# Other durations, and table loads, in the clock by which a two-block kernel lays out its background steps

## The chip, the cores and the metric

The kernel runs on one core of a Trainium2 chip. The metric is the device time of one execution in microseconds, the median of several runs. Names of engines: PE is the matrix engine (TensorE), PEld its weight loads, DVE is VectorE, ACT is ScalarE, POOL is GpSimd and SP is SyncE, which issues the transfers of the weights.

## The reference, cut to what matters

Two transformer-like blocks work one after the other on a sequence of 512 tokens with 1024 features, all in float32. A block adds a mixer and then a gated feed-forward (SwiGLU) to its input, each behind a root-mean-square norm.

```
x   : [1, 512, 1024]
first block, layer 0:  HGRN2 mixer, 8 heads of 128 keys and 128 values:
    S_t = diag(f_t) S_{t-1} + (1 - f_t) i_t^T ;  o_t = S_t^T q_t
    o = rmsnorm(o) * silu(g) ;  h = x + o @ w_out ;  h = h + swiglu(rmsnorm(h))
first block, layer 1:  dilated window attention, 12 heads in 3 groups, softmax over the groups,
    then swiglu
second block:  two mixers side by side on one input
    NSA: 8 query heads of 64 in 2 groups; three branches (compressed keys, selected blocks, window),
         each softmax(q k + mask) v, weighted by a sigmoid gate and added
    GLA: 4 heads, gated linear attention with forget factors exp(logsigmoid(.)/16)
    mix = sigmoid(m1) * (GLA out @ upg) + sigmoid(m2) * (NSA out @ upn) ;  h = h + mix @ wout2
    then swiglu
out : [512, 1024]
```

## The kernel before

**The weights.** All weight matrices pass through once, 187 MB, in units of 128 x 1024 numbers (`w_raw`). ACT casts each unit to a rounded head (`w_hi`), and the rest (`w_lo`) is a subtraction, on DVE for even units and on POOL for odd ones (line 278). A product of a weight block with an operand that is itself kept as head and rest is three matmuls of 512 columns (`mm3`): here this is called a weight product. The program has 2747 of them, and their order is fixed: HGRN's projections (operand `u`) and its output projection (`og`), feed-forward, attention, feed-forward, then the second block's projections (`u`), the products that take GLA's output (`obh`, `obl`) and those that take NSA's (`oan`), output, feed-forward.

**The background steps.** What the mixers do beside the weights (scores, decays, softmax, values) is written as generators. `spawn` puts one on a list; after every weight product `tick` lets at most one of them lay out its next step. A step's instructions on PE, DVE, ACT and POOL then stand in those engines' queues at that place for good: this is decided while the program is built.

**The clock.** `tick` asks a model of the engines, `Clock`. Every engine call goes through `Timed` (line 228, which is why each row of the trace has that line), and `Clock.issue` adds `Clock.cost` to that engine's model time, after the model times of what the instruction reads and writes, plus a hop of 0.5 us between engines (0.55 in the second block). A step is laid out only when the model says that its inputs are there:

```
        for ent in self.bg:
            if ent[1] <= now and ent[3] <= free and all(f() for f in ent[2]):
                return self.step(ent)
```

`now` is PE's model time. **Forced steps.** When a weight product needs an operand that the background has not yet made, `fetch` calls `force` until it is there. Such steps are laid out one behind the other whatever the clock says, with no weight products between them:

```
            while force and not have():
                self.force()
```

**The steps which matter here.** HGRN runs in four pairs of heads (`decay4`: tiles `Q`, `K`, `Sd`, level by level; then `decay_out`: state `St`, values `V`, squares `o_sq`, the root `hrn`, transposes `cst,o`, and `done` writes `o_n`). The output projection takes the heads in order, four output tiles at a time, so heads 6 and 7 are wanted at its 25th product. GLA runs in two pairs (`decay2`: `GQ`, `GK`, seven levels). The second block's compressed branch has steps with `Pc` and `PcT`. NSA's other two branches are 16 jobs (4 pairs of heads x 2 x 2 branches) in one generator, `nsa`: a job's scores (`ks,qs`; then DVE's maxima, and ACT's exponentials into `P`), the sums and gates onto `P` (DVE), its transposes (`cst,P`) into head and rest `PT` (ACT casts, DVE subtracts), and its value products (`PT,VV`). In a round the scores of job n are laid out, then the gates of n-1, the values of n-2, and the transposes of n-1. After every fourth job ACT copies the upper half of a bank (`pv`), DVE adds (`nsum`), POOL adds the compressed branch, and ACT casts the head of `oan`.

Of the kernel before, what the change touches and what calls it, by code (L numbers as in the profile page):

```python
# [24 lines left out]
# columns of the packed per-feature vectors  # L25
# [10 lines left out]
# columns of the constants that stay  # L36
# [9 lines left out]
# the pairs of heads before which HGRN's value products for heads 0..3 and 4..7 come  # L46
HGRN_V = {0: 0, 2: 1}
# attention's sections: the queries and keys of a head of each group, the values of a group's heads
# [4 lines left out]
def nsa_rows():  # L53
    """Feature order of the NSA heads: tile j holds head j of group 0 and head j of group 1."""
    return np.concatenate([np.arange((e * 4 + j) * 64, (e * 4 + j) * 64 + 64) for j in range(4) for e in range(2)])


def attn_heads():
    """(head of the group, group) in the order in which the output projection takes them."""
    return [(t, g) for t in range(4) for g in (1, 2)] + [(t, 0) for t in range(4)]  # L60


def weight_plan():
    """The order in which weight blocks are used: (section, [(matrix, k tile, columns)])."""
# [74 lines left out]
def plan_units(sec, chunks):  # L139
    """Cut a section's blocks into units of at most UNIT columns; the first ones are small, to start early."""  # L140
    units, cur, w = [], [], 0
    for i, ch in enumerate(chunks):
        n = len(ch[2])
        if w + n > UNIT or (sec == "hgrn" and w and i <= KD):
            units.append((cur, w))
            cur, w = [], 0
        cur.append(ch)
        w += n
    if cur:
        units.append((cur, w))  # L150
    return units
# [10 lines left out]

class Clock:
    """Rough times of the engines' queues and of the tiles' contents while the program is laid out:
    they say when a background step's inputs and banks will be there, so that TensorE isn't made to wait."""

    def __init__(self, hop):
        self.hop = hop  # from an instruction's end to the start of another engine's that waits for it
        self.free = {"pe": 0.0, "v": 0.0, "a": 0.0, "g": 0.0}
        self.written, self.read = {}, {}  # L170
        self.held = []

# [3 lines left out]
    def banks(self, now):  # L176
        """PSUM banks that are free by then."""
# [6 lines left out]
    def cost(self, eng, op, out, ins):  # L184
        n = 1
        for d in out.shape[1:]:
            n *= d
# [6 lines left out]
        if eng == "a":  # L194
            return 0.09 + n * 0.00085
        if eng == "g":
            return 0.13 + n * 0.0023
        if op == "reciprocal":
            return 0.06 + n * 0.0064
        return 0.08 + n * (0.00075 if op == "tensor_scalar" else 0.00104)  # L200

    def issue(self, eng, op, outs, ins):
# [10 lines left out]
        t += self.cost(eng, op, outs[0], ins)  # L213
# [6 lines left out]
class Timed:  # L220
# [3 lines left out]
    def __getattr__(self, op):  # L224
        f = getattr(self.eng, op)

        def call(*args, **kw):
# [6 lines left out]
            self.clock.issue(self.name, op, outs, aps + ins)  # L234
# [5 lines left out]
class Weights:  # L240
    """Streams the weights in the order of use and splits each into its float32r head and rest."""
# [70 lines left out]
class Program:  # L312
# [74 lines left out]
    def mm3(self, out, a, b, first, last):  # L387
        """out += a^T b for operands given as (head, rest)."""
# [18 lines left out]
    def gemm(self, xs, M, evac, lead=1, ms=None):  # L407
        """Feature-major product: evac(m, [128 features, 512 tokens]) for each output tile m.
        An operand may be a pair of functions: whether it is there, and what makes it."""
# [13 lines left out]
    def gemm_tok(self, n, residue=False, before=None, after=None, every=1):  # L423
        """Token-major product with n weight columns: four banks of 128 tokens, by blocks or by the rest of the token mod 4."""
# [24 lines left out]
    def norm_feed(self, k, squares=True):  # L449
        """x[k] is final: build the operand's parts and add its squares."""  # L450
# [25 lines left out]
    def sums(self, out, acc, residue=False):  # L476
        """Each token's sum over the partitions of acc, onto the token's partition."""
# [33 lines left out]
    def bcast(self, col, ps=None):  # L511
        """[128 tokens, n] to the first 128 n columns of a PSUM bank that hold every token's value on all partitions."""
# [50 lines left out]
    #  # L563
    # A head's score of query t and key s <= t is q_t . (forget factors of s+1..t) k_s. Keys and queries meet
    # block by block: when neighbouring blocks of h tokens are joined, the queries carry the factors from their
    # block's start, the keys those to their block's end and T holds each block's product, so that every factor
    # is a product of forget factors and nothing is divided.
# [5 lines left out]
    def decay4(self, Q, K, T, have, Vj, done):  # L573
        """Two heads whose values are there when have() says so, with keys K[e] [128, 512] and forget
        factors T [128, 2, 512]; Q[e] [128, 2, 512] holds head e's queries and,
        beside them, room. Blocks are joined four at a time: the room takes the queries that reach back further
        than the block before theirs, with the factors of the blocks between.
        Vj(e, j) gives head e's values of tokens 128 j.. as [tokens, 128]; done(e, o) takes the normed output,
        not yet times its gain."""
        v, a, g = self.v, self.a, self.g  # L580
        # per level: each block's product, and the products of the blocks after each of the first three
# [25 lines left out]
        def begin(e, h, T):  # L607
            """The room's queries for blocks of h tokens."""
# [57 lines left out]
    def decay2(self, Q, K, T, Vj, done):  # L666
        """Two heads on one set of keys K and forget factors T [128, 1, 512], whose queries Q [128, 2, 512] are
        zero outside each head's features. Blocks are joined two at a time."""
# [39 lines left out]
    def decay_out(self, Q, K, T, Sd, have, Vj, done):  # L708
        """Sd holds the scores within each block of 128 tokens. The blocks before come through a state
        [features, values] that is carried from block to block."""  # L710
# [49 lines left out]
    def hgrn(self):  # L760
# [16 lines left out]
        # TensorE's clock is released by activity: these run while the first operands are on their way  # L777
# [99 lines left out]
    def attn(self):  # L877
# [13 lines left out]
        def scores(gi, q, k, st):  # L891
            """Masked scores and their exponentials of one head, four blocks of 128 queries."""
# [27 lines left out]
        def merge(hg, st):  # L920
            """Softmax over the three groups' log-sum-exps, then the weighted outputs."""
# [109 lines left out]
    def block2(self):  # L1031
# [28 lines left out]
        # compressed keys and values  # L1060
# [30 lines left out]
        # gated linear attention operands  # L1091
# [25 lines left out]
        # token-major columns  # L1117
# [62 lines left out]
        # sparse attention  # L1180
# [4 lines left out]
        def rope(raw, i):  # L1185
            """Rotate, then stack the parts of the 64 features for products in two passes: q as head on one
            half of the partitions and rest on the other, k's head on both halves and k's rest on both."""
# [92 lines left out]
        def w_stage(j, e, br, P, l):  # L1280
            """Softmax's sum and the branch's gate, onto the rows of P."""
# [370 lines left out]
```

## Time and profile before

| what | value |
|---|---|
| median of 3 runs | 2163.72 us (2163.47 to 2164.20) |
| span of the profiled execution | 2162.1 us |
| PE busy | 2117.4 us, 98% |
| DVE, ACT, POOL busy | 1004.3, 783.8, 723.6 us |
| mean granted PE clock | 0.994 |

The span goes from the first to the last instruction of one profiled execution. That execution has no time of its own in the results; the runs' median is 1.6 us above the span, so 1.6 us are taken to lie around it.

### The profile page before, as it was taken

Reading aid. Unit: us, or ns where it says so; the run is one execution under the profiler, and the core shown is the slowest. Engines: PE = TensorE matmul, PEld = TensorE weight load, DVE = VectorE, ACT = ScalarE, POOL = GpSimd, SP = SyncE. Lnnn points to the kernel's source line nnn. Section 1 sums busy time; section 2 is a strip of 40 time slices with the busy share of each in tenths; the row PEclk is TensorE's granted clock in tenths of the full one; section 3 lists DMA queues with packets and bytes.
Section 4 is the critical chain, followed back from the end, with each engine's and each line's share of the span. In section 5 each row is a group of like instructions: output and inputs, shape, how many; then the busy total and the mean of one; then the engine's idle time right before and its main releaser. Section 6 shows DMA issues by size and latency. Waiting matters only on the chain.

```text
span 2162.1 us, 25412 instructions
## 1 busy us (share of the span) xinstructions
PE 2117.4 (98%) x9983; PEld 1773.4 (82%) x9983; DVE 1004.3 (46%) x1775; ACT 783.8 (36%) x1290; POOL 723.6 (33%) x442
## 2 busy tenths in 40 slices
PE   9999999999999999999999999999899999999998
PEld 7787788888888998788888888887688788888887
DVE  4778853322334555643322333447778753222322
ACT  5343443222233433443222224244455543222233
POOL 4413343323333434323322335331511253322333
PEclk9999999999999999999999999999999999999999
DMA  5111233323323222222332232321111223333332
GB/s 178 59 59 49 69 127 98 98 98 98 98 88 107 79 88 78 79 69 98 98 102 93 98 98 92 133 69 48 55 55 57 70 95 98 98 98 98 96 100 69
DMA packets 55865, 191.00 MB, mean 88 GB/s; under 512 B 6257, under 2 KB 8321, under 8 KB 55745
## 3 DMA queue, kind: packets, MB, share of 16 engines
q1 hardware_dynamic: 53584, 183.85, 26.2%
q0 software_dynamic: 1008, 3.42, 0.4%
q10 hardware_dynamic: 1152, 2.10, 0.3%
q8 instruction: 78, 1.28, 0.2%
q14 instruction: 43, 0.34, 0.1%
HBM read 187.25 MB, written 2.10 MB: 88 GB/s over the span
## 4 chain that ended last, share of the span: by engine, by line
PE 86%; DVE 9%; issue 1%; POOL 1%; ACT 1%; DMA 1%; SPq 0%; DVEq 0%; ACTq 0%; POOLq 0%
PE ps L228 86%; DVE Q L228 2%; DVE Sd L228 2%; DVE P L228 1%; DMA w_raw<-in_hgrn 1%; DVE w_lo L228 1%; DVE K L228 0%; POOL rot L228 0%; DVE Pc L228 0%; DVE qs L228 0%; POOL rs L228 0%; DVE obl L228 0%; DVE GQ L228 0%; DVE PT L228 0%; POOL w_lo L228 0%
## 5 line engine op out<-in xcount | busy, mean ns | idle before, releaser
L228 PE MATMUL ps<-u,w_hi 128*128 128x512 f32 x3392 | 1049.4, 391 | 0.0
L228 PEld LDWEIGHTS ps<-u,w_hi 128*128 128x128 f32 x3392 | 638.9, 188 | 128.9 <-issue 1.4
L228 PE MATMUL ps<-u,w_lo 128*128 128x512 f32 x1696 | 683.7, 403 | 2.2 <-POOL w_lo L228 2.2
L228 POOL TENSOR_TENSOR w_lo<-w_raw,w_hi 128x1024 fp32r<-128x1024 f32 (+2 forms) x173 | 415.8, 2403 | 745.1 <-ACT w_hi L228 636.2
L228 ACT CAST w_hi<-w_raw 128x1024 fp32r<-128x1024 f32 (+2 forms) x346 | 356.1, 1030 | 301.6 <-PE ps L228 205.4
L228 PEld LDWEIGHTS ps<-u,w_lo 128*128 128x128 f32 x1696 | 319.7, 189 | 68.3 <-issue 4.2
L228 PE MATMUL ps<-h,w_hi 128*128 128x512 f32 (+1 forms) x1078 | 326.3, 385 | 0.0
L228 DVE TENSOR_TENSOR w_lo<-w_raw,w_hi 128x1024 fp32r<-128x1024 f32 (+2 forms) x173 | 231.5, 1338 | 183.7 <-ACT w_hi L228 175.4
L228 PEld LDWEIGHTS ps<-h,w_hi 128*128 128x128 f32 x1078 | 200.9, 188 | 40.4
L228 PE MATMUL ps<-h,w_lo 128*128 128x512 f32 (+1 forms) x539 | 207.6, 385 | 0.5 <-DVE x L228 0.5
L228 POOL TENSOR_TENSOR sg<-sg,r_bc 128x512 f32<-128x512 f32 x66 | 85.8, 1299 | 290.3 <-ACT sg L228 290.3
L228 DVE TENSOR_TENSOR x<-x,ps 128x512 f32<-128x512 f32 (+1 forms) x73 | 49.5, 678 | 218.6 <-PE ps L228 218.6
L228 PE MATMUL ps<-w_hi,u 128*128 128x512 f32 (+1 forms) x448 | 139.1, 392 | 2.3 <-DVE u L228 2.3
L228 DVE TENSOR_TENSOR h<-ps,sg 128x512 f32<-128x512 f32 x66 | 45.7, 692 | 194.9 <-PE ps L228 182.4
L228 ACT ACTIVATE sg<-gs 128x512 f32<-128x512 f32 x66 | 41.7, 632 | 242.3 <-DVE gs L228 242.3
L228 ACT CAST h<-h 128x512 fp32r<-128x512 f32 x66 | 41.0, 620 | 242.8 <-DVE h L228 242.8
L228 DVE TENSOR_TENSOR gs<-ps,r_bc 128x512 f32<-128x512 f32 x66 | 45.6, 691 | 156.8 <-PE ps L228 156.7
L228 PEld LDWEIGHTS ps<-h,w_lo 128*128 128x128 f32 x539 | 101.2, 188 | 20.9 <-DVE x L228 0.7
L228 ACT ACTIVATE P<-P,nm 128x128 f32<-128x128 f32 (+2 forms) x112 | 55.2, 494 | 142.6 <-DVE nm L228 130.4
L228 POOL TENSOR_TENSOR sq_acc<-sq_acc,sq 128x512 f32<-128x512 f32 x48 | 67.2, 1405 | 117.8 <-ACT sq L228 115.7
L228 PEld LDWEIGHTS ps<-w_hi,u 128*128 128x128 f32 x448 | 95.0, 226 | 10.3 <-DVE u L228 2.7
L228 PE MATMUL ps<-w_lo,u 128*128 128x512 f32 (+1 forms) x224 | 85.8, 383 | 0.0
(294 smaller groups left out, 2231.5 us busy)
## 6 DMA issues: line engine op xcount, KB each, us to landing
w_raw<-in_ffn SPq DMA_DIRECT2D x198, 512.0 KB, 3.5
w_raw<-in_attn SPq DMA_DIRECT2D x48, 512.0 KB, 3.5
w_raw<-in_blk SPq DMA_DIRECT2D x47, 512.0 KB, 3.4
w_raw<-in_hgrn SPq DMA_DIRECT2D x36, 512.0 KB, 3.5
w_raw<-in_blk SPq DMA_DIRECT2D x7, 404.0 KB, 2.9
x<-in_xt SPq DMA_DIRECT2D x8, 256.0 KB, 5.1
w_raw<-in_hgrn SPq DMA_DIRECT2D x8, 256.0 KB, 4.0
x<-in_xt ACTq DMA_DIRECT2D x8, 256.0 KB, 5.0
```

The costliest lines, as they stand in the source:

```text
L228: r = f(*args, **kw)
```

## The change

`Clock.cost` gets other durations, and an ACT instruction whose function is of another table than the one before it costs 1.28 us more. Nothing else of the program changes; the lines that the diff empties are comments and docstrings, left out here. Both programs have the same instructions but for ACT's table loads, 46 before and 48 now, which are put in where two neighbours on ACT need different tables.

```diff
+TABLES = {AF.Exp: "exp", AF.Ln: "ln", AF.Sigmoid: "sigmoid", AF.Silu: "silu", AF.Sqrt: "sqrt"}
...
-    def cost(self, eng, op, out, ins):
-        n = 1
-        for d in out.shape[1:]:
-            n *= d
+    def cost(self, eng, op, out, ins, func=None, sums=False):
+        def size(x):
+            n = 1
+            for d in x.shape[1:]:
+                n *= d
+            return n
+
+        n = size(out)
...
         if eng == "a":
-            return 0.09 + n * 0.00085
+            t = 0.09 + n * 0.00085 + (0.092 if sums else 0)
+            if func in TABLES and TABLES[func] != self.table:
+                self.table = TABLES[func]
+                t += 1.28
+            return t
         if eng == "g":
-            return 0.13 + n * 0.0023
+            return 0.13 + n * 0.0023 if n > 256 else 0.27 + n * 0.0034
         if op == "reciprocal":
-            return 0.06 + n * 0.0064
-        return 0.08 + n * (0.00075 if op == "tensor_scalar" else 0.00104)
-
-    def issue(self, eng, op, outs, ins):
+            return 0.17 + n * 0.0064
+        if op == "tensor_reduce":
+            return 0.1 + size(ins[0]) * 0.00104
+        psum = 0.08 if any(key(x).startswith("ps_") for x in ins) else 0
+        if op == "copy_predicated":
+            return 0.2 + n * 0.00175
+        return max(0.19, psum + 0.08 + n * (0.00075 if op == "tensor_scalar" else 0.00104)) + (0.08 if sums else 0)
+
+    def issue(self, eng, op, outs, ins, func=None):
...
-        t += self.cost(eng, op, outs[0], ins)
+        t += self.cost(eng, op, outs[0], ins, func, len(outs) > 1)
...
-            self.clock.issue(self.name, op, outs, aps + ins)
+            func = next((x for x in args if isinstance(x, AF)), None)
+            self.clock.issue(self.name, op, outs, aps + ins, func)
```

Most of the new durations are longer, so most steps of HGRN, of GLA, of the compressed branch and of NSA come later among the weight products; the feed-forward sections stay as they are. Positions below are counts of weight products ahead of a step.

The first place is the end of HGRN on PE, the last head pair: values (`V,Sd`, `St,Q`), transposes (`cst,o`) and the output projection (`og`). Before, the eight products with `u` that stand ahead of the transposes end like this:

```order
L228 MATMUL ps<-u,w_lo 128x512
L228 MATMUL ps<-u,w_hi 128x512 x2
L228 MATMUL ps<-u,w_lo 128x512
L228 MATMUL ps<-u,w_hi 128x512 x2
L228 MATMUL ps<-cst,o 128x128 x8
L228 MATMUL ps<-og,w_lo 128x512
L228 MATMUL ps<-og,w_hi 128x512 x2
```

Now the same transposes stand here:

```order
L246 MATMUL ps<-V,Sd 128x128
L246 MATMUL ps<-St,Q 128x128
L246 MATMUL ps<-og,w_lo 128x512
L246 MATMUL ps<-og,w_hi 128x512 x2
L246 MATMUL ps<-og,w_lo 128x512
L246 MATMUL ps<-og,w_hi 128x512 x2
L246 MATMUL ps<-cst,o 128x128 x8
L246 MATMUL ps<-og,w_lo 128x512
```

The last value products moved from position 248 to 278, and the transposes from 256, ahead of the output projection, to 280, where they are forced; two products instead of eight lie between.

The second place is the end of NSA on PE. Before, its last value products stand among products with GLA's output, ten products ahead of the first with `oan`:

```order
L228 MATMUL ps<-obh,w_lo 128x512
L228 MATMUL ps<-obh,w_hi 128x512
L228 MATMUL ps<-obl,w_hi 128x512
L228 MATMUL ps<-PT,VV 128x512 x2
L228 MATMUL ps<-PT,VV 128x384 x2
L228 MATMUL ps<-PT,VV 128x256 x2
L228 MATMUL ps<-PT,VV 128x128 x2
L228 MATMUL ps<-obh,w_lo 128x512
L228 MATMUL ps<-obh,w_hi 128x512
L228 MATMUL ps<-obl,w_hi 128x512
```

Now the jobs' steps stand among the products with `oan` and then without any; these are the transposes of the 13th job up to those of the 14th:

```order
L246 MATMUL ps<-cst,P 128x128 x10
L246 MATMUL ps<-oan,w_lo 128x512
L246 MATMUL ps<-oan,w_hi 128x512 x2
L246 MATMUL ps<-ks,qs 128x512 x2
L246 MATMUL ps<-ks,qs 128x384 x2
L246 MATMUL ps<-ks,qs 128x256 x2
L246 MATMUL ps<-ks,qs 128x128 x2
L246 MATMUL ps<-PT,VV 128x512 x2
L246 MATMUL ps<-PT,VV 128x384 x2
L246 MATMUL ps<-PT,VV 128x256 x2
L246 MATMUL ps<-PT,VV 128x128 x2
L246 MATMUL ps<-cst,P 128x128 x10
```

Scores of the 16 jobs stood at positions 1957 to 2083, some 8.4 products apart, and now stand at 1971 to 2118, some 11 apart up to the 13th (2112); the first product with `oan` is at 2112 in both. From the scores of the 15th job to the last value products no weight product lies between (6 between the scores of the 13th and there), and the rest of `oan` follows.

The third place is ACT's queue there. Before, the casts of `oan` follow the merge gates (`mg`):

```order
L228 COPY pv<-ps 64x512
L228 ACTIVATE mg<-mg 128x1024 x2
L228 CAST w_hi<-w_raw 128x1024
L228 ACTIVATE mg<-mg 128x1024
L228 CAST oan<-nsum 128x512 x3
```

Now they follow the exponentials (`P,l`) of the 13th job, and the copy `pv` of the 12th job follows those of the 14th:

```order
L246 ACTIVATE P,l<-P,nm 128x128
L246 CAST oan<-nsum 128x512 x2
L246 CAST PT<-ps 128x512
L246 CAST PT<-ps 128x384 x2
L246 ACTIVATE P,l<-P,nm 128x512
L246 ACTIVATE P,l<-P,nm 128x384
L246 ACTIVATE P,l<-P,nm 128x256
L246 ACTIVATE P,l<-P,nm 128x128
L246 COPY pv<-ps 64x512
L246 CAST oan<-nsum 128x512
```

In GLA the first level's products moved from position 1891 to 1898 and the later ones by 6; in the compressed branch the `PcT` products moved by 5 to 17 positions.

## Rows read from the trace of the kernel before

**Rows 1.** The page, busy time of each engine.

```profile
PE 2117.4 (98%) x9983; PEld 1773.4 (82%) x9983; DVE 1004.3 (46%) x1775; ACT 783.8 (36%) x1290; POOL 723.6 (33%) x442
```

**Rows 2.** PE's waits over the span: total us, times, longest.

```profile
PE ps L228 <- DVE Q L228: 10.4, 9, 2.1
PE ps L228 <- DVE GK L228: 6.6, 3, 3.0
PE ps L228 <- DVE K L228: 3.8, 4, 1.3
PE ps L228 <- DVE PcT L228: 2.7, 3, 1.5
...
PE ps L228 <- POOL w_lo L228: 2.2, 1, 2.2
PE ps L228 <- DVE Pc L228: 1.9, 2, 1.3
PE ps L228 <- DVE P L228: 1.8, 3, 1.3
```

**Rows 3.** Windows: length, busy PE, PEld, DVE, ACT, POOL, PE clock, DMA.

```profile
181.30:184.50 3.20, 3.20 (x10) 2.91 (x10) 3.10 (x9) 0.00 (x0) 0.00 (x0) 0.50 0.30 120
1457.90:1464.50 6.60, 6.07 (x22) 5.52 (x23) 6.47 (x11) 0.00 (x0) 0.10 (x1) 0.50 0.32 94
1550.00:1553.30 3.30, 3.30 (x10) 2.52 (x11) 3.20 (x6) 2.14 (x3) 1.74 (x2) 0.50 0.47 159
```

**Rows 4.** The chain that ended last, its longest stretch.

```profile
250.18 610.29 PE ps L228 x2771
```

**Rows 5.** Timeline of HGRN's end: start, duration, engine, operation.

```profile
268.84 0.39 PE L228 MATMUL ps<-St,Q 128*128 128x128 f32 x2
...
270.71 1.28 ACT L228 ACT_TABLE_LOAD   x1
272.00 0.30 ACT L228 ACTIVATE hrn<-hst,eps 128x8 f32<-128x8 f32 x1
...
274.55 1.03 PE L228 MATMUL ps<-cst,o 128*128 128x128 f32 x8
```

**Rows 6.** Windows, the stretch of GLA's levels, columns as in rows 3.

```profile
1449.00:1485.00 36.00, 29.33 (x166) 23.71 (x165) 35.15 (x60) 2.85 (x4) 10.71 (x15) 0.91 0.14 44
```

**Rows 7.** Timeline of GLA's levels.

```profile
1455.48 2.52 POOL L228 TENSOR_TENSOR w_lo<-w_raw,w_hi 128x1024 fp32r<-128x1024 f32 x1
1455.83 2.45 DVE L228 TENSOR_TENSOR GK<-GK,GF 128x256 f32<-128x256 f32 x1
...
1470.55 0.43 DVE L228 TENSOR_TENSOR GK<-GK,T 128x256 f32<-128x256 f32 x1
```

**Rows 8.** Timeline of a job of NSA: scores, maxima, exponentials, gates.

```profile
1629.46 1.38 PE L228 MATMUL ps<-ks,qs 128*128 128x512 f32 x8
1630.12 0.69 DVE L228 CUSTOM_DVE_ANT_0 P<-ps,cst 128x512 f32<-128x512 f32 x1 [0.24 <-PE ps L228]
...
1632.09 0.73 ACT L228 ACTIVATE P<-P,nm 128x512 f32<-128x512 f32 x1 [3.68 <-DVE nm L228]
...
1632.37 1.27 DVE L228 TENSOR_SCALAR P<-P,l 128x512 f32<-128x512 f32 x4
...
1634.29 1.03 ACT L228 CAST w_hi<-w_raw 128x1024 fp32r<-128x1024 f32 x1
```

**Rows 9.** Timeline of NSA's last job: transposes, rests, `pv`, POOL's sum, the cast.

```profile
1710.09 1.28 PE L228 MATMUL ps<-cst,P 128*128 128x128 f32 x10 [1.25 <-DVE P L228]
...
1711.37 1.62 DVE L228 TENSOR_TENSOR PT<-ps,PT 128x512 fp32r<-128x512 f32 x3 [0.23 <-ACT PT L228]
...
1716.07 0.58 ACT L228 COPY pv<-ps 64x512 f32<-64x512 f32 x1 [2.07 <-PE ps L228]
...
1717.44 2.34 POOL L228 TENSOR_TENSOR nsum<-nsum,oa 128x512 f32<-128x512 f32 x1 [7.59 <-DVE nsum L228]
...
1725.90 0.61 ACT L228 CAST oan<-nsum 128x512 fp32r<-128x512 f32 x1
```

More of the change, by code (lines that the diff above doesn't have):

```diff
@@ L171, in __init__ @@
         self.held = []
+        self.table = None
     def ready(self, tiles):
```

## The prediction

> **What bounds the kernel now.** I read the page's busy times first: PE works 2117.4 us, 98% of the span [rows 1], so the time is that of PE's work plus its waits, and a change of order can only move the waits (and what the clock loses after them). The second view is the list of PE's waits [rows 2]. Apart from single ones at the norms, they fall on four places: HGRN's levels (`Q` 10.4 and `K` 3.8 us), GLA's levels (`GK` 6.6), the compressed branch (`PcT` 2.7, `Pc` 1.9, and a `w_lo` on POOL 2.2 that stands beside it) and NSA's jobs (`P` 1.8). The third is the granted clock by windows: after waits in three of these places PE ran at 0.50, the lower of its two levels (1.2 instead of 2.4 GHz), for 3.2, 6.6 and 3.3 us [rows 3]. Work done at half clock takes twice as long, so each of these cost about half its length: 1.6, 3.3 and 1.65 us. The fourth is the chain that ended last: its longest stretch is 2771 matmuls in 610.29 us, 0.220 us each [rows 4], so a weight product, three of them, is 0.66 us of cover for a step's inputs.
>
> So the most that the change can take away is 14.2 + 1.6 us in HGRN, 6.6 + 3.3 in GLA and 6.8 + 1.65 in the compressed branch, 34.2 us together. What it can cost lies where later steps run into the weight product that needs them: there the clock isn't asked and the steps are forced. The order shows two such places.
>
> **HGRN.** From the second pair of heads on the steps stand 13 to 30 products later and further apart. 13 products are 8.6 us, against a longest wait of 2.1 [rows 2], so I take the 14.2 and the 1.6 as gone, 15.8, but for three remainders. The first pair moves by only 2 products, 1.3 us: of its waits, estimated at 2.4 as a sixth of 14.2, 1.1 stay. Collisions like the one in the next part, which no duration per instruction covers, keep an estimated 3 (bounds 0 and 8). And the end is forced. In the profile the last value products begin at 268.84 and the transposes that follow from them at 274.55 [rows 5]; between them lie the squares, a table load of 1.28, the root, the reciprocal and two products on DVE. Of these 5.7 us the weight products that lay between covered everything. Now two products, 1.3 us, lie between; the remaining 4.4 would be a wait if ACT and DVE did the same in between as before. But there is no gate work left for them at that point, so I take 2.5. Behind the transposes the gain (ACT), the gate (DVE) and the cast (ACT) must run before the next `og` product, each about as long as the cast of 512 columns, 0.61 [rows 9]: 1.8, and with the hand-overs 2.0. So 4.5 (bounds 3 and 8). HGRN: -15.8 + 1.1 + 3 + 4.5 = **-7.2** (bounds -12 and +1).
>
> The table load is where a page and a row differ. The load takes 1.28 us and ACT's next instruction starts at 272.00, 0.01 us behind it [rows 5]. The Trainium skill, ScalarE: Activation LUTs, section What ACT_TABLE_LOAD costs, adds a drain of about 1.38 us to each switch; by that the forced end would be 5.9 instead of 4.5. The row decides, and 4.5 stands.
>
> **GLA.** In the 36.0 us of its levels DVE works 35.15 [rows 6]. Each level waits for the products of DVE of the level before, so here DVE and not the order sets the pace. What helps is that the first level now stands 7 products, 4.6 us, later: the first wait, 3.0 [rows 2], goes. The later levels move by the same 6 products, so their distance to each other stays, and so do the other 3.6 us and, somewhere, the 3.3 of the clock. **-3.0** (bounds 0 and -9.9).
>
> **Compressed branch.** The products with `PcT` stand 5 to 17 weight products later, 3 us or more, against a longest wait of 1.5; 8.45 us are there to be had. I leave 2.0 for POOL's `w_lo`, whose unit isn't moved: **-6.5** (bounds -8.5 and -2).
>
> **NSA's end.** Here the new order costs. The first product with `oan` stays at position 2112, but at that point the scores of four jobs are still to come, and only 6 weight products lie among what is left. PE's waits, from the rows of one job:
> - Ahead of `oan`'s first product. Its cast now stands behind the exponentials of the 13th job. From a job's scores to its exponentials are 1632.09 - 1629.46 = 2.63 us, the exponentials end at 1634.29, 2.20 later [rows 8], the cast is 0.61 [rows 9]: 5.44, of which PE spends 1.38 on the scores. Wait 4.1.
> - Ahead of `oan`'s third operand. The copy `pv` of the 12th job stands behind the exponentials of the 14th: 2.63 + 2.20 = 4.83, less PE's scores and value products of 1.38 each, leave 2.1. From the copy to POOL's sum are 1717.44 - 1716.07 = 1.37, the sum takes 2.34 at most here and I take 1.9, and the cast is 0.61 [rows 9]. Wait 6.0.
> - From there to the last value products all hangs on DVE and the hand-overs: a job's transposes to the last of its rests take 1711.37 + 1.62 - 1710.09 = 2.9 [rows 9], the maxima to the weighted `P` 1632.37 + 1.27 - 1630.12 = 3.5 [rows 8]. Four of the first (13th to 16th job) are 11.6, two of the second 7.0, the last job's gates 1.5, and the copy `pv` of the 14th job, behind the exponentials of the 16th, holds up DVE's add and what is queued behind it by about 1.5: 21.6. PE's own work in it is two `oan` products, 1.3, four transposes of 1.28 and five scores and values of 1.38: 13.3. Wait 8.3.
> - Ahead of `oan`'s last operand: copy, add, POOL's sum and cast once more, with nothing else on POOL: 1.37 + 1.6 + 0.61 = 3.6.
>
> Together 22.0 (bounds 15, if the hand-overs overlap better than in one queue, and 30, if each round waits for all of the one before). Waits of 4 to 8 us are longer than those after which the clock fell (2.1 to 3.0 us), so I add 3.5, the half of some 7 us at half clock, twice an episode of rows 3 (bounds 0 and 9). The waits for `P`, 1.8, go. NSA: 22.0 + 3.5 - 1.8 = **+23.7** (bounds 13 and 37).
>
> Attention's steps move by some products and none is forced; the feed-forward sections stay; both at nothing, since PE has no waits for them but single ones at the norms. The two more table loads lie on ACT, 36% busy [rows 1].
>
> **The sum.** -7.2 - 3.0 - 6.5 + 23.7 = +7.0. The profiled span is 2162.1, so the new one is 2169.1; with the 1.6 us by which the runs' median lies above the span, **2170.7 us**.
>
> **Rivals.**
> *The front gives all that it can* (faster): no collision keeps a wait in HGRN, GLA's late start takes away all of its waits and the clock's fall, and the compressed branch's go too: -15.8 + 1.1 + 4.5 - 9.9 - 8.5 = -28.6, and with the end of NSA as above -4.9: 2158.8. For it speaks that each single wait is shorter than the 4 us and more by which most steps move; against it GLA's DVE. It decides as long as the end of NSA costs less than 24.
> *The two sides cancel* (the same): the end of NSA at its lower part, 17, against 16.7 at the front: 2164. For it: my four waits at the end are added up one after the other, and ACT's exponentials may hide in them.
> *The clock stays low through the end of NSA*: PE works there some 24 us in 45, and at half clock those take 24 more, of which what lies beside DVE is hidden; half of it beyond the 3.5 is +8.5: 2179. For it: after 3.00 us of waiting it stayed low for 6.6 [rows 3], the longest of the three. Against it: work comes between all of the waits.
> *DVE's durations are still too short* (slower): the new model gives a multiplication of 128x256 0.35 us where the undisturbed row has 0.43, and 2.45 was measured beside a POOL subtraction of 2.52 [rows 7]. If this keeps half of HGRN's waits, +7.1: 2178. Of the same pair, the Trainium skill, SBUF — State Buffer, section Who interferes with whom, says that a DVE instruction with two SBUF inputs and a GpSimd read of SBUF share a port pair as an exclusive lock, so that one blocks for the other's whole length; the trace agrees (2.45 against 0.43), and by that rule a collision returns wherever the moved steps meet a `w_lo` on POOL.
>
> **How the numbers follow.** 0.2% of the time, 4.3 us, is about what can be told from no change here: faster is below 2159.4, slower above 2168.0. The forecast has 0.40, all of it slower for its own range of 2168 to 2175; the low clock and the short durations 0.10 each, slower; the cancelling case 0.22, the same; the front giving all 0.18, faster. That is 0.18, 0.22 and 0.60. The range reaches from the faster rival to the slower ones: 2157 to 2181. Its bounds are not the sum of all bounds, of which one side's extremes would have to come together.
>
> **What the new profile would show.** Right: in the list of PE's waits `Q` and `K` together below 6 us instead of 14.2; waits on `oan`, `PT` and `P` of together about 22 us between the first `oan` product and the last; a wait of 2 to 3 us ahead of HGRN's last transposes and one of about 2 on `og` behind them; a lowered clock at NSA's end. GLA's stretch still has DVE busy nearly throughout. Wrong: waits at NSA's end of 15 us or less, which would make it the same or faster; `Q` or `GK` waits of before's size, by which it gets slower than forecast; or new waits on `w_hi` or `w_lo`, if the moved steps hold up the splitting of the weights in ACT's and DVE's queues, which I have put at nothing.

## The result, and where the time went

The changed kernel takes 2189.71 us (median of 4 runs, 2188.06 to 2190.09) against 2163.59 for the kernel before (4 runs, 2163.1 to 2164.2): ratio 1.0121, 95% interval 1.0106 to 1.0135. The forecast was 2170.7, in a range from 2157 to 2181. The direction was right, the size was not: +26.1 us instead of +7.

The profiled execution has a span of 2187.8 us, 25.7 more than before. By the page PE's work grew by about what half clock makes of it, and the rest are waits:

```profile
PE 2126.4 (97%) x9983; PEld 1779.6 (81%) x9983; DVE 998.3 (46%) x1775; ACT 787.7 (36%) x1292; POOL 717.7 (33%) x442
```

PE is busy 9.0 us longer than in [rows 1] with the same 9983 matmuls, and idle 16.7 us longer. The list of PE's waits over the span, which answers to [rows 2], says where (total us, times, longest):

```profile
PE ps L246 <- ACT oan L246: 14.8, 3, 6.0
PE ps L246 <- POOL w_lo L246: 11.5, 3, 6.4
PE ps L246 <- DVE P L246: 5.2, 3, 2.5
...
PE ps L246 <- DVE o L246: 2.5, 1, 2.5
PE ps L246 <- DVE PT L246: 2.4, 2, 2.2
PE ps L246 <- DVE hrn L246: 2.3, 1, 2.3
PE ps L246 <- DVE GK L246: 2.1, 4, 0.6
PE ps L246 <- DVE Pc L246: 1.7, 1, 1.7
PE ps L246 <- ACT og L246: 1.6, 1, 1.6
...
PE ps L246 <- DVE Q L246: 1.3, 1, 1.3
...
PE ps L246 <- DVE og L246: 0.7, 1, 0.7
...
PE ps L246 <- DVE K L246: 0.5, 1, 0.5
```

HGRN's `Q` and `K` fell from 14.2 to 1.8 us, as forecast, and `GK` from 6.6 to 2.1, which is more than forecast. But `w_lo` from POOL, 2.2 before, is now 11.5, and `oan` and `P`, under 3 before, are 20.0. The windows at half clock answer to [rows 3] (length, busy PE, PEld, DVE, ACT, POOL, PE clock, DMA); each begins where PE works again after a wait, or within 1.1 us of it:

```profile
283.30:288.70 5.40, 5.38 (x13) 4.20 (x14) 1.90 (x3) 1.56 (x2) 2.38 (x1) 0.50 0.01 2
1456.30:1459.50 3.20, 3.20 (x14) 2.91 (x14) 1.51 (x4) 0.00 (x0) 1.24 (x1) 0.50 0.94 346
1546.90:1555.00 8.10, 8.10 (x18) 4.80 (x19) 3.20 (x6) 7.44 (x11) 4.01 (x4) 0.50 0.28 86
1708.50:1712.10 3.60, 3.58 (x9) 2.79 (x9) 2.82 (x8) 0.49 (x1) 0.00 (x0) 0.50 0.00 0
1724.00:1729.10 5.10, 5.06 (x17) 4.33 (x18) 2.41 (x4) 2.48 (x4) 0.00 (x0) 0.50 0.00 0
1739.90:1742.80 2.90, 2.88 (x12) 2.60 (x13) 1.65 (x3) 2.68 (x8) 0.00 (x0) 0.50 0.00 0
1752.10:1756.40 4.30, 4.30 (x10) 3.42 (x11) 3.08 (x4) 0.52 (x1) 1.83 (x2) 0.50 0.34 93
```

Together 32.6 us, so about 16.3 are lost to the clock, 9.7 more than the 6.55 of before. (Both traces also have some 3 us at half clock near 30 us from the start, and some at the very end; these are left out.) Waits and clock by place, after less before:

| place | waits | half clock | sum | forecast |
|---|---|---|---|---|
| HGRN | 8.9 - 14.5 | 2.7 - 1.6 | -4.5 | -7.2 |
| attention | 3.0 - 0.2 | 0 | +2.8 | 0 |
| GLA | 2.1 + 4.4 - 6.6 | 1.6 - 3.3 | -1.8 | -3.0 |
| compressed branch | 1.7 + 6.4 - 6.8 | 4.05 - 1.65 | +3.7 | -6.5 |
| NSA's end | 20.2 - 2.8 | 7.95 - 0 | +25.4 | +23.7 |
| together | | | +25.6 | +7.0 |

The sum is within 0.1 of the spans' difference, but not because each row is that good. (HGRN's 14.5 are `Q` and `K` with 0.3 for `Sd`; 4.4 and 6.4 are the two long waits for `w_lo`, ahead of positions 1897 and 1961; 2.8 at NSA's end is `P`, 1.8, and one wait on `oan`. A wait for `u` at the first norm, 0.7 longer now, is left out.)

A second count does without waits: when PE starts the same weight product in the two traces. At the five products below PE has the same work behind it in both.

| weight product | before | after | added on the way there | forecast |
|---|---|---|---|---|
| 64, ahead of HGRN's steps | 54.96 | 55.60 | +0.6 | |
| 320, behind HGRN | 318.95 | 313.20 | -6.4 | -7.2 |
| 1872, behind attention, ahead of GLA | 1429.79 | 1426.68 | +2.6 | 0 |
| 1934, behind GLA | 1518.78 | 1515.03 | -0.6 | -3.0 |
| 2144, behind the compressed branch and NSA | 1745.81 | 1771.95 | +29.9 | +17.2 |

So HGRN gained 1.9 us more than its waits and clock account for, GLA gained next to nothing, and the last stretch cost a little more; the errors of the first table's rows cancel in its sum. The half clock also scatters between executions: behind attention's wait for `PT`, 2.2 us long in both, PE ran on at full clock in this trace and at half clock in that of experiment 4.

**NSA's end** went as the order said. PE's rows of the timeline, from the 13th job's scores on only those that wait:

```profile
1701.64 1.38 PE L246 MATMUL ps<-ks,qs 128*128 128x512 f32 x8
1708.52 0.80 PE L246 MATMUL ps<-oan,w_lo 128*128 128x512 f32 x1 [5.51 <-ACT oan L246]
...
1724.04 0.80 PE L246 MATMUL ps<-oan,w_lo 128*128 128x512 f32 x1 [5.96 <-ACT oan L246]
...
1733.38 1.29 PE L246 MATMUL ps<-cst,P 128*128 128x128 f32 x10 [1.68 <-DVE P L246]
...
1739.92 2.37 PE L246 MATMUL ps<-cst,P 128*128 128x128 f32 x10 [2.49 <-DVE P L246]
...
1745.10 1.31 PE L246 MATMUL ps<-cst,P 128*128 128x128 f32 x10 [1.03 <-DVE P L246]
...
1752.08 0.80 PE L246 MATMUL ps<-oan,w_lo 128*128 128x512 f32 x1 [3.38 <-ACT oan L246]
```

The four waits of the forecast (4.1, 6.0, 8.3 and 3.6) are 5.5, 6.0, 5.2 and 3.4.

**The compressed branch** did not. PE waits 6.35 us for a `w_lo` that POOL does at its place in the queue. The rows of POOL and DVE ahead of it:

```profile
1537.83 0.73 POOL L246 TENSOR_TENSOR Pc<-Pc,cst 128x256 f32<-128x256 f32 x1
...
1538.59 1.50 DVE L246 TENSOR_TENSOR Pc<-Pc,cl 128x256 f32<-128x256 f32 x1 [0.70 <-POOL Pc L246]
...
1540.10 1.39 DVE L246 TENSOR_TENSOR qs<-rot,qs 64x512 fp32r<-64x512 f32 x2
...
1541.52 0.69 DVE L246 TENSOR_TENSOR rot<-ps,tab 128x512 f32<-128x512 f32 x1
...
1542.36 1.69 POOL L246 TENSOR_TENSOR rot<-rot,rot 128x512 f32<-128x512 f32 x1 [2.55 <-DVE rot L246]
...
1544.02 2.79 POOL L246 TENSOR_TENSOR w_lo<-w_raw,w_hi 128x1024 fp32r<-128x1024 f32 x1
...
1546.86 0.80 PE L246 MATMUL ps<-u,w_lo 128*128 128x512 f32 x1 [6.35 <-POOL w_lo L246]
```

`w_lo` itself needs only its cast. It stands behind `rot`, which waits 2.55 us for DVE; DVE comes to it behind `Pc` and `qs`, and `Pc` had waited for POOL. `Pc` also takes 1.50 us here, beside POOL's next `rot`; a row of the same form took 0.43 at 1525.91, with POOL idle. Further up the chain that ends in this `w_lo`, `Pc` took 1.47 us and four `ks` 6.36, both beside POOL's work; at 0.43 us a `Pc` and at the 0.70 of one `qs` above, which is of the same form as `ks` and had POOL idle, the three would together be 5.7 us shorter. That is an estimate of what such collisions add here: no run takes them away, and the kernel before has them in this stretch too (`ks` 3.79, `Pc` 2.57). In GLA it is plainer still: POOL's rows up to this `w_lo` are the same in both kernels, some 3 us earlier now, and PE, which has no products of the levels ahead of it now, comes to it 10.1 us earlier (1455.26 instead of 1465.39, although it waits).

```profile
1447.46 2.88 POOL L246 TENSOR_TENSOR T<-T 128x128 f32<-128x128 f32 x6
...
1451.65 1.26 POOL L246 TENSOR_TENSOR rot<-rot,rot 128x512 f32<-128x512 f32 x1
...
1452.87 4.67 POOL L246 TENSOR_TENSOR w_lo<-w_raw,w_hi 128x1024 fp32r<-128x1024 f32 x2
...
1455.26 0.50 PE L246 MATMUL ps<-u,w_lo 128*128 128x512 f32 x1 [4.38 <-POOL w_lo L246]
```

Before, the same `w_lo` ran from 1455.48 to 1458.00 [rows 7] and nobody waited for it, because PE stood at `GK` for its 3.0 us [rows 2] until 1458.43.

### The profile page after: what moved, and what is told of

The parts are those of the page before. It is cut to its first block, busy times and chain, and to the rows that moved or that the text cites. A ratio compares the mean times of both kernels' runs of the same rounds, so it can differ in the third digit from the quotient of the medians.

```text
span 2187.8 us, 25406 instructions
## 1 busy us (share of the span) xinstructions
PE 2126.4 (97%) x9983; PEld 1779.6 (81%) x9983; DVE 998.3 (46%) x1775; ACT 787.7 (36%) x1292; POOL 717.7 (33%) x442
## 3 DMA queue, kind: packets, MB, share of 16 engines
q8 instruction: 78, 1.28, 0.2%
## 4 chain that ended last, share of the span: by engine, by line
PE 88%; DVE 6%; ACT 3%; POOL 1%; issue 1%; DMA 1%; ACTq 0%; SPq 0%; DVEq 0%; POOLq 0%
PE ps L246 88%; DVE P L246 1%; DVE Sd L246 1%; DVE Q L246 1%; DMA w_raw<-in_hgrn 1%; ACT P L246 0%; ACT w_hi L246 0%; DVE PT L246 0%; DVE w_lo L246 0%; ACT L246 0%; POOL w_lo L246 0%; ACT mg L246 0%; DVE og L246 0%; POOL T L246 0%; DVE GQ L246 0%
## 5 line engine op out<-in xcount | busy, mean ns | idle before, releaser
L246 PE MATMUL ps<-u,w_lo 128*128 128x512 f32 x1696 | 683.1, 403 | 11.5 <-POOL w_lo L246 11.5
L246 DVE TENSOR_TENSOR w_lo<-w_raw,w_hi 128x1024 fp32r<-128x1024 f32 (+2 forms) x173 | 235.9, 1363 | 200.9 <-ACT w_hi L246 186.4
```

The costliest lines, as they stand in the source:

```text
L246: r = f(*args, **kw)
```

## The experiments

All are timed against the kernel before, whose median in the groups of runs was 2163.4 to 2163.7. Where a kernel uses the durations of before for a part, `cost` has them behind a flag that is set at the place named.

**1. New durations in the first block only.** `self.clock.hop = 0.55` marks the second block's start.

```diff
         self.clock.hop = 0.55
+        self.clock.old = True
```

> New durations for the first block, those of before for the second. In the two traces PE reaches the second block 3.1 us earlier after the change than before it. Theory A (the loss arises in the second block alone, where steps run into the products that need them): 2160.5 us, and the second block's waits are those of before. Rival B (the lead of 3 us is used up by waits that come later anyway, such as that for w_lo on POOL): 2163 to 2164.

Measured: 2160.18 us, ratio 0.9986 (0.9978 to 0.9995). Theory A. The first block gives 3 us, and all of the loss arises in the second: in this trace the stretch from product 1872 to 2144 is 0.5 us shorter than before, in the changed kernel's 29.2 longer.

**2. Durations of before for NSA only.**

```diff
+                    self.clock.old = True
                     self.spawn(nsa())
```

> New durations up to the point where NSA's generator is put on the list, those of before from there on. The jobs then end at position 2112 and none is forced. Theory A (NSA's forced end costs about 26 us): 2163 to 2167, with waits of together under 4 us on oan, P and PT and the clock high there; the waits for w_lo on POOL at positions 1897 and 1961 stay. Rival B (most of the loss is made ahead of NSA, by GLA and the compressed branch): 2175 or more.

Measured: 2166.05 us, ratio 1.0013 (1.0004 to 1.0022). Theory A: without the forced end 23.7 of the 26.1 us are gone. PE's waits at NSA's end (1690 to 1760 us):

```profile
PE ps L261 <- ACT oan L261: 1.2, 1, 1.2
PE ps L261 <- DVE P L261: 0.4, 1, 0.4
```

Two more are of 0.2 us. Of the two waits for `w_lo` that theory A left standing, that at 1897 is still 4.35 us; that at 1961 is 1.4, and waits of 3.2 and 2.0 us for a `w_lo` from DVE stand at 1953 and 1969 instead.

Experiments 1 and 2 differ by 5.9 us, and only GLA, the compressed branch and NSA's place behind them differ in their programs: the new durations cost there, where I had forecast a gain of 9.5. In the traces the stretch from product 1872 to 2144 is 4.3 us longer in experiment 2 than in experiment 1. The flag takes in some of the compressed branch: its steps behind NSA's start also have the durations of before, and its last product with `PcT` stands at 1980 here, at 1992 in the changed kernel and at 1975 before.

**3. Two late units on DVE.**

```diff
-            (self.g if u % 2 else self.v).tensor_sub(...)
+            (self.g if u % 2 and u not in (241, 249) else self.v).tensor_sub(...)
```

> The changed kernel, with the rests w_lo of two units (those first used at positions 1897 and 1961) subtracted on DVE instead of POOL. Theory A (these units are late because they stand behind other work in POOL's queue): both waits, 4.4 and 6.4 us, go, and with them the half clock behind them (about 1.7 and 4.1 us); DVE's own lateness gives back up to half: 2175 to 2183. Rival B (DVE is as late as POOL, since both wait for each other's results): 2187 or more, with waits for w_lo from DVE or for GK and PcT in their place.

Measured: 2186.37 us, ratio 1.0112 (1.0098 to 1.0126). Each theory holds at one place. At 1897 the wait for `w_lo` is gone, and one of 2.34 us for `GK` stands a little further on; no half clock follows. At 1961 PE waits as before, now for DVE:

```profile
PE ps L246 <- DVE w_lo L246: 5.4, 1, 5.4
```

So in GLA it was POOL's queue, and in the compressed branch DVE's queue is as late as POOL's. Part of the gain is given back at NSA's end, where the wait ahead of `oan`'s first product is 7.8 us instead of 5.5.

**4. `oan` split when its sum is laid out**, in calls that the clock doesn't book, so that PE's order stays.

```diff
                     g.tensor_add(oan[j], oan[j], oa[j])
+                    hi, lo = self.pair("oan")
+                    nc.scalar.copy(hi, oan[j])
+                    nc.vector.tensor_sub(lo, oan[j], hi.bitcast(F32))
+                    oas[j] = hi, lo
                     ready.append(j)
...
-            return self.split(oan[j], "oan")
+            return oas[j]
```

> The changed kernel, with oan split into head and rest as soon as its sum is laid out, not when a product asks for it; the order on PE is the same. Theory A (ahead of oan's first product PE waits for a cast that stands behind the exponentials of the 13th job): that wait, 5.5 us, goes, with some of the half clock behind it: 2181 to 2185; the wait of 6.0 on oan's third operand stays within 1 us. Rival B (the end of NSA goes at DVE's pace, so PE only waits elsewhere): 2187 or more.

Measured: 2190.74 us, ratio 1.0127 (1.0112 to 1.0143): the time of the changed kernel, as theory B said. The wait named did go (`oan` 9.9 us in 2 instead of 14.8 in 3), but the casts and subtractions stand earlier in ACT's and DVE's queues now, and other steps came late; the longest of PE's waits from 1640 to 1760 us:

```profile
PE ps L246 <- ACT oan L1341: 9.9, 2, 6.4
PE ps L246 <- DVE P L246: 5.4, 5, 2.5
```

With 2.6 us on `mg` and `PT` these are 17.9 us against 20.2, so the waits alone gave 2. Between products 1934 and 2144 little of it is left (+29.7 against the kernel before, the changed kernel +29.9); why is not shown. Elsewhere, where this edit moves nothing, half clock cost more in this execution than in the changed kernel's: GLA's stretch at half clock is 6.8 us long instead of 3.4, and attention has one (length, busy PE, PEld, DVE, ACT, POOL, PE clock, DMA) that the changed kernel's trace lacks:

```profile
877.28:880.69 3.41, 3.41 (x12) 2.73 (x11) 1.13 (x2) 1.65 (x2) 2.82 (x2) 0.50 0.21 85
```

So the 1.0 us by which this run lies above the changed kernel say nothing.

**5. Matmuls of ones in the waits at NSA's end**, into a bank that nothing else uses then (ahead of the transposes, into their bank before they overwrite it).

```diff
+        def spin(ps, n):
+            for _ in range(n):
+                self.mm(ps, self.ones, self.ones)
...
+            n = (34, 0, 36, 20)[j]
+            if n:
+                spin(self.ps()[:, 0:128], n)
```

> The changed kernel with added matmuls of ones, whose result nothing reads, in PE's queue ahead of the waits at NSA's end: 34 ahead of oan's first product, 36 and 20 ahead of its third and fourth operand, 10 ahead of the transposes of the last three jobs. They fill waits that are there anyway. Theory A (the half clock behind the waits lengthens the chain, by about 8 us): the clock stays high at NSA's end and the time is 2181 to 2186. Rival B (PE's work lies beside DVE's there, so its clock costs little): 2188 to 2191.

Measured: 2189.06 us, ratio 1.0114 (1.0100 to 1.0128). Inconclusive: the clock did stay at 1.00, but the added work ran for 7.8 and 8.3 us where 5.5 and 6.0 were to be filled. Experiment 9 mends it.

**6. New durations in HGRN only.**

```diff
         self.hgrn()
+        self.clock.old = True
```

> New durations in HGRN alone; from its end on those of before, which gives the order of before. Theory A (HGRN gives 4 to 6 us net, attention's moved steps cost 2.6): 2157.5 to 2159.5, that is 1 to 3 us below the run with new durations in the whole first block. Rival B (attention's loss isn't due to its moved steps): 2160 to 2161.

Measured: 2156.42 us, ratio 0.9968 (0.9956 to 0.9980), a little better than theory A's range. So HGRN's part is -7.3 us, which is the forecast's -7.2. The run is 3.8 below experiment 1, from which only attention's steps differ; in the traces the difference between products 320 and 1872 is 2.6. PE's waits in attention (860 to 930 us) in the changed kernel are

```profile
PE ps L246 <- DVE PT L246: 2.2, 1, 2.2
PE ps L246 <- POOL w_lo L246: 0.8, 1, 0.8
```

and one of 1.3 for `ao` that was there before. Attention's moved steps, which I had put at nothing, cost some 3 us.

**7. The same, with the masked copies at their old duration.**

```diff
-        if op == "copy_predicated":
-            return 0.2 + n * 0.00175
```

> As the run with new durations in HGRN alone, but with the old duration for the masked copies into Sd (copy_predicated). HGRN's last value products then stand at 263 and its last transposes at 272, so that no step is forced. Theory A (the forced end costs 2.5 + 2.3 us of waits and 2.7 of half clock, and the levels' waits stay away because the other durations are long enough): 2152 to 2156. Rival B (the long masked copies are what keeps the levels' waits away): 2159 to 2164, with waits for Q and K back.

Measured: 2161.85 us, ratio 0.9990 (0.9981 to 0.9999). Theory B. PE's waits in HGRN (69 to 275 us):

```profile
PE ps L261 <- DVE Q L261: 5.4, 6, 1.6
PE ps L261 <- ACT St L261: 3.0, 1, 3.0
PE ps L261 <- DVE K L261: 1.7, 2, 1.2
```

No step is forced, but 7.1 of the levels' 14.2 us are back: the masked copy's longer duration is what keeps half of them away. Two things weaken this. The 3.0 us for `St` are none of the levels': ACT's copy stands behind its loads of `x` (last section). And the trace is of the fastest of the eleven executions, 3.6 us below their median, so it shows only part of the loss.

**8. No table loads, no charge for PSUM or an accumulator on DVE.**

```diff
-            if func in TABLES and TABLES[func] != self.table:
+            if False and func in TABLES and TABLES[func] != self.table:
...
-        psum = 0.08 if any(key(x).startswith("ps_") for x in ins) else 0
+        psum = 0.0 if any(key(x).startswith("ps_") for x in ins) else 0
...
-        return max(0.19, ...) + (0.08 if sums else 0)
+        return max(0.19, ...) + 0
```

> The changed kernel without two of its new charges: no table loads, and neither the 0.08 us for a PSUM source nor that for an accumulator on DVE. NSA's scores then stand some 8 positions apart, the 16th at 2103, and only the last job's values (at 2118) are forced. Theory A (these charges, too long for instructions that follow each other on one engine, push NSA's jobs into oan): 2164 to 2172. Rival B (the loss has to do with the order ahead of NSA): 2180 or more.

Measured: 2173.58 us, ratio 1.0043 (1.0029 to 1.0057), 1.6 above theory A's range. 16 of the 26 us go with these charges, 13.3 of them between products 1872 and 2144 by the traces, the others ahead of GLA. They were taken out together, so the run doesn't say which of them it is. `oan` still makes PE wait 8.4 us (5.0 and 3.4), since the last job's values are forced. GLA's steps stand where they stood before; in the compressed branch the wait for `w_lo` at 1961 is gone, and one of 6.6 us for `Pc` stands two products ahead of that place.

**9. Experiment 5 with a fill that fits.**

```diff
-            n = (34, 0, 36, 20)[j]
+            n = (22, 0, 24, 13)[j]
```

(and 6 instead of 10 ahead of the transposes)

> As the run with added matmuls at NSA's end, with fewer of them: there they lasted 7.8, 8.3 and 4.7 us ahead of oan's operands and 2.4 ahead of the last transposes, longer than the waits (5.5, 6.0, 3.4 and 1.0 to 2.5) that they were to fill. Now 22, 24 and 13, and 6. Theory A (half clock costs about 8 us there, and the too long fill had eaten the gain): the clock stays high or nearly so and the time is 2181 to 2185. Rival B (the clock costs little there): 2187 to 2190.

Measured: 2185.41 us, ratio 1.0101 (1.0087 to 1.0115), 4.3 below the changed kernel and just outside theory A's range. From the 13th job's scores to `oan`'s last operand, windows of the changed kernel and of this one:

```profile
1701.64:1752.08 50.44, 30.09 (x149) 25.19 (x148) 29.25 (x92) 23.97 (x59) 4.11 (x3) 0.81 0.05 19
```

```profile
1699.92:1747.13 47.21, 43.00 (x304) 37.76 (x302) 28.98 (x92) 23.57 (x59) 4.11 (x3) 1.00 0.05 19
```

With the clock at 1.00 throughout, the stretch is 3.2 us shorter although PE does 155 matmuls more. The 4.3 us of half clock behind the stretch (2.2 us) go as well.

**10. New durations for NSA only**, the counterpart of experiment 2.

```diff
+                    self.clock.old = False
                     self.spawn(nsa())
```

> One part of the change alone: the durations of before up to the point where NSA's generator is put on the list, the new ones from there on. Its last jobs are forced as in the changed kernel. Theory A (NSA's forced end costs 25 us by itself): 2185 to 2192. Rival B (it costs so much only because GLA and the compressed branch are late as well): below 2180.

Measured: 2192.38 us, ratio 1.0132 (1.0117 to 1.0148), 0.4 above theory A's range. By the medians NSA's part of the change alone costs 29 us, more than the whole change. In the trace 2.4 of these arise ahead of HGRN, where the program is that of before, and 26.9 between products 1934 and 2144. The flag takes in the compressed branch's later steps too, among which PE waits 3.6 us for `Pc`.

**11. New durations in HGRN up to its gate's projection.**

```diff
+        self.clock.old = True
         self.gemm(self.u, 8, evac_g)
```

> New durations in HGRN up to the gate's projection (the last eight output tiles before the output projection), those of before from there on. HGRN's last value products stand at 268 and its last transposes at 274, ahead of the 280 at which they would be forced. Theory A (the forced end of HGRN costs about 6 us, and the steps ahead of the gate are those that profit from later places): 2150 to 2154. Rival B (ACT's queue, held by the loads of x, or DVE's levels make PE wait ahead of the last steps instead): 2156 to 2160.

Measured: 2150.51 us, ratio 0.9941 (0.9929 to 0.9954). Theory A, and faster than both kernels. PE's waits in HGRN (69 to 290 us), 14.5 before and 8.9 after the whole change:

```profile
PE ps L261 <- DVE K L261: 2.4, 1, 2.4
PE ps L261 <- DVE Q L261: 1.5, 2, 1.3
```

**12. The compressed branch's mask product on DVE**, booked on POOL as before so that the order stays.

```diff
-            g.tensor_mul(P, P, cmul)
+            nc.vector.tensor_mul(P, P, cmul)
+            self.clock.issue("g", "tensor_mul", [P], [P, cmul])
```

> The changed kernel, with the compressed branch's mask product (Pc times its mask, 0.7 us on POOL) done on DVE instead; the clock still books it on POOL, so the order stays. In the chain of the changed kernel the late w_lo at position 1961 hangs on work that goes from ACT to POOL to DVE and back, in which the mask product on POOL stands behind two other products there. Theory A (w_lo is late because POOL's and DVE's queues hold each other up): the wait for w_lo at 1961, 6.4 us, falls by 2 to 4 and the time is 2184 to 2187.5. Rival B (the queues are late by their own work, and DVE only gets more of it): 2188.5 to 2192, with the wait as long as before.

Measured: 2186.93 us, ratio 1.0112 (1.0095 to 1.0129). The time is in theory A's range, but not for its reason: the wait of 1.7 us for `Pc` is gone, while the one for `w_lo` at 1961 is 6.5 us, as rival B said. The mask product isn't what holds `w_lo` up. POOL's `rot` ahead of it still waits 2.1 us for DVE (2.55 in the rows above); taking that apart was not tried.

## Why the prediction was wrong, step by step

**What bounds the kernel** was right: the same matmuls, and the time is waits and clock.

**NSA's end** was right in its mechanism, its places and its waits (20.2 us against 22.0). Experiment 2 takes this part away: between products 1934 and 2144 its trace is 26.0 us below the changed kernel's. Experiment 10 leaves it nearly alone: 26.9 us. The forecast was 23.7. Of its two terms the clock's was mis-sized: 3.5 us, after "twice an episode", where four episodes of 3.6, 5.1, 2.9 and 4.3 us cost 7.95. Experiment 9 gives 4.3 of these back with the clock held up, so the larger part of it does lie on the path. The point that it takes DVE's pace, not PE's, to price the forced jobs holds as well, but the middle part (8.3) was 3.1 too dear, and the first wait (4.1) 1.4 too cheap: the maxima of the 13th job began 2.1 us behind its scores (1703.71 and 1701.64) instead of 0.7, behind the rests of the 12th job's `PT` and a product of `mg` on DVE.

**The compressed branch** is the step that failed: "8.45 us are there to be had", of which I took 6.5, and it became +3.7 by waits and clock, and +3.9 between products 1934 and 2144 in experiment 2, where NSA's end costs next to nothing. Moving a step past its longest wait takes away the wait for that step. I read from that that PE would not wait, but PE then runs on into the next thing that the same late queues owe it, here `w_lo`. I had named this among what would make the prediction wrong and put it at nothing, without looking at what stood ahead of each `w_lo` on POOL; the wait of 2.2 in [rows 2], at this very position, was the sign. Experiment 3 shows that the same unit on DVE is as late, so the place has no free engine to move it to; experiments 2 and 8, in which the steps stand a few products elsewhere, have waits of 3.2 us for DVE's `w_lo` and 6.6 for `Pc` there. How much of the lateness the collisions of DVE and POOL make is open: experiment 12 ruled out only the mask product.

**GLA** failed at the same step. The first wait for `GK` went, as forecast, and 4.4 us for `w_lo` came in its place, which experiment 3 puts on POOL's queue. By waits and clock it still gained 1.8 of the 3.0 us, but from product 1872 to 1934 it is only 0.6 us faster than before, and so are the traces of experiments 1, 6, 7, 8, 10 and 11 (0.6 to 1.5), in which GLA's steps stand as before: later steps gave nothing here. Experiments 1 and 2 show that GLA and the compressed branch together cost 4 to 6 us under the new durations, instead of giving 9.5.

**HGRN** was right in mechanism and in size: -6.4 by PE's starts, -7.3 by experiment 6. Its forced end, 2.5 and 2.0 by forecast, is 2.5 and 1.6 + 0.7, by the rows on `o` and `og`. ACT's root follows the table load at once, as in [rows 5]:

```profile
277.81 1.28 ACT L246 ACT_TABLE_LOAD   x1
279.10 0.30 ACT L246 ACTIVATE hrn<-hst,eps 128x8 f32<-128x8 f32 x1
```

So the drain of which the Trainium skill speaks (ScalarE: Activation LUTs, What ACT_TABLE_LOAD costs) costs nothing here. Of the first pair's waits 1.3 us stayed, where I had 1.1. Behind the first pair 0.5 us for `K` and 2.3 for `hrn` are left, where I kept 3 for collisions. The second is a collision, although the list names the reciprocal `hrn`: ACT's root for it had ended at 243.78, and the reciprocal stands on DVE behind a product on `K` that takes 2.72 us beside POOL's `w_lo`, where the same form took 0.55 with POOL idle:

```profile
247.31 0.55 DVE L246 TENSOR_TENSOR K<-K,KT 128x384 f32<-128x384 f32 x1
...
251.55 2.55 POOL L246 TENSOR_TENSOR w_lo<-w_raw,w_hi 128x1024 fp32r<-128x1024 f32 x1
...
251.79 2.72 DVE L246 TENSOR_TENSOR K<-K,KT 128x384 f32<-128x384 f32 x1
```

What was left out is the half clock behind the forced end (2.7 us). One reading of the order was wrong without harm: the levels' products of the first pair stand 0 to 16 weight products later, not 2, and those of the other pairs 3 to 39, not 13 to 30.

**Attention**, put at nothing because no step of it is forced, costs 2.6 to 3.8 (the traces and experiment 6): one product meets a `PT` that DVE makes too late, and one a `w_lo` on POOL.

**The rivals.** That DVE's durations are too short was no cause in HGRN: `Q` and `K` waits went. Experiment 8 points the other way at NSA, where charges that were added are too long. One sign of it: a maximum over 512 columns on DVE lasts 0.69 us, but the next one starts 0.62 behind it (1729.71 and 1730.33 in the changed kernel's timeline), where the new duration is 0.08 + 0.08 + 512 x 0.00104 + 0.08 = 0.77. That the low clock lasts through NSA's end was half right: it was low in four episodes, not throughout, and cost 4.5 more than the 3.5 in the sum.

## What to carry to other kernels

A list of waits names what PE stood at, not what it would have stood at next: before a wait is booked as a gain, look at what else is due from the same queues, above all work that everything needs (here the weights' rests), and at what stands ahead of it there. A planner that lays out steps by a clock needs a due time as well: durations that are a little too long add up from job to job, and steps that miss their due time are laid out in one block with nothing beside them. A wait costs its length and, where the clock falls, half of the stretch at half clock behind it; both belong in the sum. A list of waits is itself a rough sum: the times at which PE starts the same product in both traces show what each stretch really gained or lost.

## What the hardware showed that I had not expected

Waits of 5.5, 6.0, 2.5 and 3.4 us were each followed by 2.9 to 5.1 us at half clock, and filling them with matmuls that nothing needs kept the clock at 1.00 over 47 us and made the kernel 4.3 us faster. A wait of 2.34 us in experiment 3, at GLA, was not followed by a lower clock, and attention's wait of 2.2 us was in some traces (experiments 2, 4 and 12) and not in others. And ACT's transfers count in its queue: in experiment 7 it issued the eight loads of `x` from 261.48 to 268.98, and the copy into `St`, which stands behind them, came after 6.92 us in which ACT did nothing else.

```profile
269.02 0.43 ACT L261 COPY St<-ps 128x128 f32<-128x128 f32 x2 [6.92 <-DMA x<-in_xt]
```
